# Thirteen tiny DRAM-to-DRAM copies ahead of the loads of a streaming pooling kernel

## The chip, the cores and the metric

The kernel runs on one core of one Trainium2 chip. A core has several engines with instruction queues of their own; this kernel uses ScalarE (ACT in the profile), VectorE (DVE) and SyncE (SP), and 16 DMA engines that move data between DRAM and the on-chip memory. The metric is the device time of one execution in microseconds. Three runs of the kernel before took 394.58, 394.63 and 394.68 us; the median is 394.63 us.

## The reference

The input `x` has the shape 32 x 256 x 4096 in 32-bit floats (134.2 MB), and the output 32 x 256 x 1024 (33.6 MB). Every four neighbouring elements of the last axis give one output, the root of the mean of their squares (p is 2, the window is 4 wide, and windows do not overlap):

```python
for i in range(out_length):
    window = np.abs(x[:, :, i * 4:i * 4 + 4]) ** p
    result[:, :, i] = np.mean(window, axis=-1) ** (1.0 / p)
```

## The kernel before

The whole input is treated as one long row of numbers. It is cut into seven blocks, and each block into 128 equal rows, one for each partition of the on-chip memory. A block's rows are read by up to four loads, of 13184 columns each (52736 bytes for each partition, 6592 KB in all); there are 20 loads, numbered 0 to 19, the last one a little narrower. Three input tiles (`xt`, 128 x 13184) are used in turn, so load i+3 goes into the tile that load i held.

What is done with a load: ScalarE squares it in place in two halves (`square`, L101). VectorE adds pairs (`pairs`, L107) and then the pair sums (`fours`, L111), which leaves a quarter of the columns in a PSUM tile (`st`). ScalarE takes the root of it with a scale of 1/4 (`root`, L114) into the output tile `ot`. When all the loads of a block are done, one store (L98) writes `ot` to the block's rows of the output. The roots of a load come between the squares of the next one. The last two loads are cut finer, so that little is left to do when the last data arrive.

The order on each engine is the order of the Python program (`manual_schedule`): the framework adds the waits and moves nothing. Loads are issued by SP, in order. Load i+3 is issued when the sums of load i are done, since it overwrites them. The stores of the first four blocks are issued by ACT from its own instruction stream, the last three by SP. So two DMA queues are in use: q1 holds what SP issued, and q10 what ACT issued.

Load 0 is split. Its first 1024 columns (`EARLY`) are issued by ACT and the other 12160 by SP. Loads 1 and 2 follow at once on SP and wait for nothing. ACT then runs a table load and a root of a one-column tile, `first`, and waits for load 0.

One thing is not seen in the source. The framework gives each DMA one of eight completion semaphores, in the order of the program and across both queues (the built program names them DMAHW0 to DMAHW7). A DMA that takes a semaphore again first makes its issuing engine wait until the last DMA on that semaphore has completed. In the kernel before, the first eight DMAs (the two parts of load 0, loads 1 to 5 and the first store) each take a fresh one. Every later reuse comes long after the earlier DMA has landed.

Of the kernel before, what the change touches and what calls it, by code (L numbers as in the profile page):

```python
# [1 line left out]

# [4 lines left out]


@with_exitstack
def kernel(  # L10
    ctx: ExitStack,
    tc: tile.TileContext,
    x: bass.AP,
    p: float,
    kernel_size: int,
    out: bass.AP,
):

    nc = tc.nc

    assert float(p) == 2.0, "kernel specialized for p == 2"
    k = int(kernel_size)  # L30
    assert k == 4, "kernel specialized for kernel_size == 4"

    P = nc.NUM_PARTITIONS
    fp32 = mybir.dt.float32
    Act = mybir.ActivationFunctionType
    add = mybir.AluOpType.add
    xf = x.rearrange("b c l -> (b c l)")
    of = out.rearrange("b c l -> (b c l)")
    total = xf.shape[0] // P

    W = 13184
    H, R = W // 2, W // k
    X_SLOTS = 3
    EARLY = 1024
    LAST = total - 19 * W
    widths = [W] * 19 + [LAST]
    n = len(widths)
    assert 0 < LAST <= W and LAST % 16 == 0


    blocks = [[0, 1, 2, 3], [4, 5, 6, 7], [8, 9, 10, 11], [12, 13], [16, 17, 14, 15], [18], [19]]
    block_of = {i: b for b, loads in enumerate(blocks) for i in loads}
    block_width = [sum(widths[i] for i in loads) for loads in blocks]

    x_pool = ctx.enter_context(tc.tile_pool(name="x_pool", bufs=1))
    o_pool = ctx.enter_context(tc.tile_pool(name="o_pool", bufs=1))
    s_pool = ctx.enter_context(tc.tile_pool(name="s_pool", bufs=1, space=bass.MemoryType.PSUM))
    x_tiles = [x_pool.tile([P, W], fp32, name=f"xt{j}") for j in range(X_SLOTS)]
    o_tile = o_pool.tile([P, 4 * R], fp32, name="ot")
    first = o_pool.tile([P, 1], fp32, name="first")  # L60
    s_tiles = [s_pool.tile([P, 2048], fp32, name=f"st{j}") for j in range(2)]
    ctx.enter_context(tc.manual_schedule())

    def rows(flat, b, div):
        at = sum(block_width[:b]) * P // div
        return flat[at:at + block_width[b] * P // div].rearrange("(p w) -> p w", p=P)


    place = {}
    for b, loads in enumerate(blocks):  # L70
        for q, i in enumerate(loads):
            if i < 18:
                place[i] = o_tile[:, q * R:(q + 1) * R]
    free = x_tiles[17 % X_SLOTS]
    place[18] = free[:, 0:R]
    place[19] = free[:, R:R + LAST // k]

    xs = {}

    def load(i):  # L80
        b = block_of[i]
        at = sum(widths[j] for j in blocks[b][:blocks[b].index(i)])
        xs[i] = x_tiles[i % X_SLOTS][:, 0:widths[i]]
        cuts = [0, widths[i]] if i else [0, EARLY, W]
        queues = [nc.sync] if i else [nc.scalar, nc.sync]
        for queue, c, e in zip(queues, cuts, cuts[1:]):
            queue.dma_start(out=xs[i][:, c:e], in_=rows(xf, b, 1)[:, at + c:at + e])  # L87

    def store(b, queue):
        if b <= 2:  # L90
            held = o_tile[:, :]
        elif b == 3:
            held = o_tile[:, 0:2 * R]
        elif b == 4:
            held = o_tile[:, :]
        else:
            held = place[blocks[b][0]]
        queue.dma_start(out=rows(of, b, k), in_=held)  # L98

    def square(v):  # L100
        nc.scalar.activation(out=v, in_=v, func=Act.Square)  # L101

    def pairs(v):

        q = v.rearrange("p (n j) -> p n j", j=k)
        h = v[:, 0:v.shape[1] // 2].rearrange("p (n j) -> p n j", j=2)
        nc.vector.tensor_tensor(out=h, in0=q[:, :, 0:2], in1=q[:, :, 2:4], op=add)  # L107

    def fours(o, v):
        h = v[:, 0:v.shape[1] // 2].rearrange("p (n j) -> p n j", j=2)  # L110
        nc.vector.tensor_tensor(out=o, in0=h[:, :, 0], in1=h[:, :, 1], op=add)  # L111

    def root(o, s):
        nc.scalar.activation(out=o, in_=s, func=Act.Sqrt, scale=1.0 / k)  # L114

    def roots(i):
        for c in range(2):
            root(place[i][:, c * R // 2:(c + 1) * R // 2], s_tiles[c][:, 0:R // 2])
        if i in (3, 7, 11, 13):
            store(block_of[i], nc.scalar)  # L120

    for i in range(X_SLOTS):
        load(i)

    nc.vector.memset(first[:, :], 1.0)  # L125
    root(first[:, :], first[:, :])
    for i in range(18):
        halves = [xs[i][:, c * H:(c + 1) * H] for c in range(2)]
        waits = i > 1 and (i - 1) % 4 == 0
        square(halves[0])  # L130
        if i and not waits:
            roots(i - 1)
        square(halves[1])
        if waits:
            roots(i - 1)
            for v in halves:
                pairs(v)
            for c, v in enumerate(halves):
                fours(s_tiles[c][:, 0:R // 2], v)
        else:  # L140
            for c, v in enumerate(halves):
                pairs(v)
                fours(s_tiles[c][:, 0:R // 2], v)
        if i + X_SLOTS < n:
            load(i + X_SLOTS)
    roots(17)


    c = 5560
    v = xs[18][:, 0:c]  # L150
    nc.vector.tensor_tensor(out=v, in0=v, in1=v, op=mybir.AluOpType.mult)  # L151
    square(xs[18][:, c:W])
    store(4, nc.sync)
    for a, b in ((0, c), (c, W)):
        pairs(xs[18][:, a:b])
        fours(place[18][:, a // k:b // k], xs[18][:, a:b])
    ends = [0, 6912, 10064, LAST]
    for a, b in zip(ends, ends[1:]):
        v = xs[19][:, a:b]
        o = place[19][:, a // k:b // k]  # L160
        square(v)
        if a == 0:
            root(place[18], place[18])
            store(5, nc.sync)
        pairs(v)
        fours(o, v)
        if a:
            root(*last)
        last = (o, o)
    root(*last)  # L170
    store(6, nc.sync)


# [1 line left out]
_INS = ['x', 'p', 'kernel_size']  # L175
_OUTS = [((32, 256, 1024), 'float32')]

_NUMBERS = {'p': 2.0, 'kernel_size': 4}


# [26 lines left out]
```

## Time and profile before

| what | value |
|---|---|
| median of the three runs | 394.63 us |
| span of the profiled execution, first to last instruction | 392.7 us |
| runs' median less this span | 1.9 us |
| ScalarE busy | 279.3 us (71% of the span) |
| VectorE busy | 223.4 us (57%) |
| q1, SP's DMAs | 143.62 MB, 84.9% of the 16 DMA engines' time |
| q10, ACT's DMAs | 24.15 MB, 14.2% |

The profiled execution has no separate time but its span; the runs stand 1.9 us above it, and that is what lies around the first and last instruction. A line of the profile gives engine busy time, a group of equal instructions with its mean duration, or, for DMA, the packets of a queue and the time that they took as a share of 16 engines' time. A window of the profile restricts such a view to a stretch of the span, with times in us from the span's start. A packet is counted in the window in which it starts. In this kernel a packet is one partition's row of one DMA, or the 4-byte write that reports the end of a DMA on one DMA engine.

### The profile page before, as it was taken

How to read it: one execution, taken by the hardware profiler on the slowest of the kernel's cores; microseconds unless marked ns; L12 is line 12 of the kernel's file. 1: busy time of each engine (PE TensorE's matmuls, PEld its weight loads, DVE VectorE, ACT ScalarE, POOL GpSimd, SP SyncE). 2: the span in 40 equal slices, each digit the busy share in tenths (PEclk: the TensorE clock that was granted, in tenths of full speed). 3: DMA queues.
4: the chain of work that ended last, by engine and by line, in shares of the span. 5: the costliest groups of instructions: out<-in, count | busy, mean ns of one | idle time of the engine just before them, and what ended most of it. 6: DMA issues, size and time to landing. Idle time of an engine off the chain costs nothing.

```text
span 392.7 us, 311 instructions
## 1 busy us (share of the span) xinstructions
DVE 223.4 (57%) x84; ACT 279.3 (71%) x82; POOL 0.2 (0%) x4
## 2 busy tenths in 40 slices
DVE  0046586766460567664606667645166654669992
ACT  1095988987650999876419898773297929897792
POOL 0000000000000000000000000000000000000000
DMA  8999999999999999999999999999999999999997
GB/s 337 436 430 430 430 440 440 435 457 376 430 430 430 446 430 440 430 440 440 446 430 436 435 435 431 435 430 430 430 430 419 457 414 430 435 429 451 415 428 320
DMA packets 4034, 167.79 MB, mean 427 GB/s; under 512 B 448, under 2 KB 448, under 8 KB 576
## 3 DMA queue, kind: packets, MB, share of 16 engines
q1 hardware_dynamic: 3312, 143.62, 84.9%
q10 hardware_dynamic: 720, 24.15, 14.2%
q14 instruction: 2, 0.02, 0.0%
HBM read 134.22 MB, written 33.55 MB: 427 GB/s over the span
## 4 chain that ended last, share of the span: by engine, by line
DMA 73%; ACT 17%; DVE 6%; issue 2%; SPq 0%; ACTq 0%; DVEq 0%
DMA xt<-in_x_dram 46%; DMA out_dram<-ot 27%; ACT xt L101 12%; ACT ot L114 5%; DVE xt L107 3%; DVE st L111 2%; DVE xt L111 1%; ACT xt L114 1%; SPq L87 0%; ACTq L101 0%; DVEq L107 0%; ACTq L114 0%
## 5 line engine op out<-in xcount | busy, mean ns | idle before, releaser
L101 ACT ACTIVATE xt<-xt 128x6592 f32<-128x6592 f32 (+4 forms) x40 | 221.4, 5547 | 61.2 <-DMA xt<-in_x_dram 59.6
L107 DVE TENSOR_TENSOR xt<-xt 128x3296 f32<-128x3296 f32 (+5 forms) x41 | 143.1, 3489 | 125.0 <-ACT xt L101 124.7
L111 DVE TENSOR_TENSOR st<-xt 128x1648 f32<-128x1648 f32 x36 | 67.4, 1882 | 36.0 <-ACT ot L114 34.1
L114 ACT ACTIVATE ot<-st 128x1648 f32<-128x1648 f32 x36 | 53.5, 1536 | 43.1 <-DMA out_dram<-ot 40.3
L111 DVE TENSOR_TENSOR xt<-xt 128x1390 f32<-128x1390 f32 (+4 forms) x5 | 7.3, 1452 | 0.2
L114 ACT ACTIVATE xt<-xt 128x3296 f32<-128x3296 f32 (+3 forms) x4 | 6.0, 1492 | 1.1 <-DVE xt L111 1.1
L151 DVE TENSOR_TENSOR xt<-xt 128x5560 f32<-128x5560 f32 x1 | 5.9, 5942 | 0.0
L114 ACT ACT_TABLE_LOAD x1 | 1.3, 1283 | 1.2 <-PEq L188 1.2
L125 DVE MEMSET first<- 128x1 f32 x1 | 0.1, 59 | 0.8 <-PEq L188 0.8
L114 ACT ACTIVATE first<-first 128x1 f32<-128x1 f32 x1 | 0.2, 202 | 0.0
L188 POOL MEMSET const-bfloat16-1.0<- 128x1 bf16 x1 | 0.1, 102 | 0.0
L188 POOL MEMSET const-uint8-127<- 128x1 uint8 x1 | 0.1, 102 | 0.0
L188 POOL MEMSET const-float32-0.0<- 128x1 f32 x1 | 0.1, 99 | 0.2 <-issue 0.2
L188 POOL MEMSET const-float32-1.0<- 128x1 f32 x1 | 0.1, 99 | 0.0
## 6 DMA issues: line engine op xcount, KB each, us to landing
xt<-in_x_dram SPq DMA_DIRECT2D x18, 6592.0 KB, 34.0
out_dram<-ot ACTq DMA_DIRECT2D x3, 6592.0 KB, 35.4
out_dram<-ot SPq DMA_DIRECT2D x1, 6592.0 KB, 24.8
xt<-in_x_dram SPq DMA_DIRECT2D x1, 6080.0 KB, 18.7
xt<-in_x_dram SPq DMA_DIRECT2D x1, 5824.0 KB, 25.2
out_dram<-ot ACTq DMA_DIRECT2D x1, 3296.0 KB, 27.7
out_dram<-xt SPq DMA_DIRECT2D x1, 1648.0 KB, 10.5
out_dram<-xt SPq DMA_DIRECT2D x1, 1456.0 KB, 5.8
```

Of the source, the lines that this page charges most:

```text
L101: nc.scalar.activation(out=v, in_=v, func=Act.Square)
L107: nc.vector.tensor_tensor(out=h, in0=q[:, :, 0:2], in1=q[:, :, 2:4], op=add)
L111: nc.vector.tensor_tensor(out=o, in0=h[:, :, 0], in1=h[:, :, 1], op=add)
L114: nc.scalar.activation(out=o, in_=s, func=Act.Sqrt, scale=1.0 / k)
L125: nc.vector.memset(first[:, :], 1.0)
L151: nc.vector.tensor_tensor(out=v, in0=v, in1=v, op=mybir.AluOpType.mult)
L188: nc = _bacc.Bacc("TRN2", target_bir_lowering=False, num_devices=1)
```

## The change

Load 0 is no longer split: SP issues all its 13184 columns as one DMA. Ahead of the loads ACT issues thirteen copies from `x` straight to the output in DRAM. The copy with n lines (n from 4 to 16) takes 128 columns (512 bytes) from each of the first n rows of the input's first block and writes them to n rows of the output's first block. The columns differ from copy to copy. The store of that block, much later, overwrites all these places with the results, and waits for the copies that it overwrites.

```diff
-    EARLY = 1024
+    TOUCH = 128
...
-        cuts = [0, widths[i]] if i else [0, EARLY, W]
-        queues = [nc.sync] if i else [nc.scalar, nc.sync]
-        for queue, c, e in zip(queues, cuts, cuts[1:]):
-            queue.dma_start(out=xs[i][:, c:e], in_=rows(xf, b, 1)[:, at + c:at + e])
+        nc.sync.dma_start(out=xs[i], in_=rows(xf, b, 1)[:, at:at + widths[i]])
...
+    def touch(lines):
+        to = rows(of, 0, k)[0:lines, (lines - 1) * TOUCH:lines * TOUCH]
+        nc.scalar.dma_start(out=to, in_=rows(xf, 0, 1)[0:lines, (lines - 1) * TOUCH:lines * TOUCH])
+
+    for lines in range(4, 17):
+        touch(lines)
     for i in range(X_SLOTS):
         load(i)
```

There are now sixteen DMAs ahead of everything else, so the eight semaphores are used twice there. The built program orders them as follows (copy n is the copy with n lines). Copy 4 takes DMAHW0, load 0 takes DMAHW1, copies 5 to 10 take DMAHW2 to DMAHW7. Copy 11 takes DMAHW0 again, and ACT waits for copy 4 before it issues it. Copy 12 takes DMAHW1, and ACT waits for load 0. Copies 13 to 16 take DMAHW2 to DMAHW5 behind copies 5 to 8. Load 1 takes DMAHW6, and SP waits for copy 9. Load 2 takes DMAHW7, and SP waits for copy 10. The order of the instructions on VectorE and on the other engines is unchanged.

## The prediction

> **What bounds the kernel now.** I read the page first: the busy shares, the 40 slices and the queues.
>
> ```profile
> span 392.7 us, 311 instructions
> DVE 223.4 (57%) x84; ACT 279.3 (71%) x82; POOL 0.2 (0%) x4
> DMA  8999999999999999999999999999999999999997
> GB/s 337 436 430 430 430 440 440 435 457 376 430 430 430 446 430 440 430 440 440 446 430 436 435 435 431 435 430 430 430 430 419 457 414 430 435 429 451 415 428 320
> q1 hardware_dynamic: 3312, 143.62, 84.9%
> q10 hardware_dynamic: 720, 24.15, 14.2%
> ```
>
> The two queues together fill 99.1% of the 16 DMA engines' time. No compute engine is near that. A change moves the end if it adds DMA work, leaves the DMA engines without work, or takes away one of the few places where they run slowly. Such places stand in the DMA view, in windows that hold just one row for each of the 16 engines. The first below is the start, the second an undisturbed stretch at 90 us, the third the moment when the first store joins the loads (ACT issued it at 90.42).
>
> ```profile
> DMA packets 16, 0.78 MB, mean 324 GB/s; under 512 B 0, under 2 KB 0, under 8 KB 0
> q1 hardware_dynamic: 16, 0.78, 103.2%
> ```
>
> ```profile
> DMA packets 16, 0.84 MB, mean 703 GB/s; under 512 B 0, under 2 KB 0, under 8 KB 0
> q1 hardware_dynamic: 16, 0.84, 162.9%
> ```
>
> ```profile
> DMA packets 16, 0.84 MB, mean 703 GB/s; under 512 B 0, under 2 KB 0, under 8 KB 0
> q1 hardware_dynamic: 16, 0.84, 224.5%
> ```
>
> The windows are 1.7 to 4.1, 89.95 to 91.15 and 91.9 to 93.1 us. A share times the window's length is the time of one row: 103.2% of 2.4 is 2.48 us for the first rows (48640 bytes), 162.9% of 1.2 is 1.95 us for an undisturbed row (52736 bytes), 224.5% of 1.2 is 2.69 us for the rows beside the first store's start. So the start stretches the first row by 0.68 us (at the undisturbed rate 48640 bytes take 1.80), and the first store costs each engine about 0.74 us, once: later stores show no such stretch.
>
> Next, how two queues share an engine, in the window from 4.2 to 17.5 us, where ACT's part of load 0 (4096-byte rows) and SP's run together:
>
> ```profile
> q1 hardware_dynamic: 112, 5.45, 94.7%
> q10 hardware_dynamic: 111, 0.45, 8.3%
> ```
>
> 112 rows of q1 and 111 of q10: an engine takes one packet from each queue in turn, though those of q10 are twelve times smaller. One of them takes 8.3% of 16 x 13.3 us over 111, which is 0.16 us.
>
> Last the timeline of the start, and SP's waits up to 40 us:
>
> ```profile
> 0.73 0.41 ACTq L87 DMA_DIRECT2D xt<-in_x_dram  x1
> 0.73 36.08 SPq L87 DMA_DIRECT2D xt<-in_x_dram  x4
> 1.17 1.28 ACT L114 ACT_TABLE_LOAD   x1 [1.17 <-PEq L188]
> 2.47 0.20 ACT L114 ACTIVATE first<-first 128x1 f32<-128x1 f32 x1
> 19.59 11.28 ACT L101 ACTIVATE xt<-xt 128x6592 f32<-128x6592 f32 x2 [16.92 <-DMA xt<-in_x_dram]
> ```
>
> ```profile
> SPq L87 <- DMA xt<-in_x_dram: 17.5, 1, 17.5
> ```
>
> SP issues loads 0, 1 and 2 back to back from 0.73 us. It then waits for load 0 (the 17.5 us) and for its sums, and issues load 3 at about 36.4. Loads 1 and 2 are thus in q1 long before load 0 has landed, and the engines go from one to the next without a hole.
>
> **The change, part by part.**
>
> *The early piece goes.* Its 8 rows on each engine cost 0.16 us each against 4096 / 52736 x 1.95 = 0.15 within a longer row, and one report packet less: about -0.1 us on every engine.
>
> *The copies as DMA work.* No row of before is a 512-byte copy. From below one costs its bytes at the row rate, 0.02 us; from above the 0.16 us of a 4096-byte row. I take 0.03, near the lower end, since it is an eighth of that row. 130 data packets and as many reports over 16 engines are 8 of each for an engine: +0.3 us (0.2 to 1.4). An engine that gets all 13 copies pays 0.4. What comes before load 1 on an engine is paid inside the hole described next; I count 0.1.
>
> *Load 1's new wait.* This is the largest term. Load 1 takes the completion semaphore of copy 9, so SP issues it only when copy 9 has landed, and load 2 stands behind it on SP. ACT issues copies 4 to 10 at 0.41 us each, from 0.73 to about 3.6, so all of them are in the rings when load 0's first rows end at 4.2 to 5.2 us. If copy n lies on n engines, one row each, and always from the same first engine, the first four engines hold all of them: up to copy 9, six data packets and six reports, 12 packets. Alternating with load 0's eight rows and its report, they need more turns than load 0 offers. Copy 9 then ends just behind load 0 on these engines. Before, the reports of load 0 fall between 17.98 and 19.02 us by engine, 18.35 in the mean, and the first four engines, which start first, are among the earliest, at 18.0 to 18.25. So copy 9 is written at about 18.35. From report to waiting engine: the last report of load 0 starts at 19.02 and ACT starts at 19.59, and two later loads show 0.4 to 0.5; I take 0.45. SP issues load 1 at 18.8. From issue to first packet the start shows 1.02 us (0.73 to 1.75); the first rows then start over 0.9 us, 1.3 us after the issue in the mean, and are stretched by 0.68. An engine is back at full rate, counted as if at once, at 18.8 + 1.3 + 0.7 = 20.8 us, where before it went on at 18.35: +2.45 us. Nothing covers this, for q1 holds only load 0 until then. Bounds: 1.3 if the second start shows no stretch and no spread of starts; 3.2 if copies stretch the first engines by as much as the first store does (0.74), since all engines then wait for these four.
>
> *ACT's new waits.* Copy 12 waits for load 0, at about 19.5. Behind it on ACT stand four more copies, the table load, the root of `first` and the first square. Five issues of 0.34 to 0.41, 1.28 and 0.20: the square starts at about 22.9 instead of 19.59. VectorE follows, and load 3's issue goes from 36.4 to 39.7. Load 2's rows keep the engines busy until about 52, and load 1 lands only at about 37, when ACT is done with load 0 (34.3). Cost nothing; if the cover were gone it would be 3.3 us. The waits of loads 3 to 7 for copies 11 to 16 end long before, as these drain within some ten rows, by about 41.
>
> *The first store's stretch.* The copies write to the output before it, on every engine. If the stretch belongs to the first write to that tensor, up to 0.74 us goes at 92 us, less what the copies pay for it. If it belongs to reading `ot`, nothing goes. I take half, -0.4 (0 to -0.74). Later waits for stores and loads shift with the loads.
>
> Sum: -0.1 + 0.1 + 2.45 - 0.4 = +2.05 us against the profiled 392.7; the 1.9 us around the span stay, so 394.63 becomes 396.7.
>
> The Trainium skill, "DMA: Bandwidth & Descriptors", section "Queues, rings and completion order", says that an engine drains a packet of about 9 to 17 descriptors from one ring before it turns to the next. By that the copies would be through after a row or two, load 1 would be issued in time, and the sum would lose its 2.45. The alternation above, one row each, speaks against it. Section "Why a DMA increments its semaphore by 16 and not by 1" of the same page gives a DMA of n rows from SP or ACT the lowest-numbered n engines for such n; no row here shows that, and it speaks for the wait as I counted it.
>
> **The rivals.**
>
> *No hole.* The copies get through earlier: their first engine moves on from copy to copy, so that the 39 rows of copies 4 to 9 give an engine two or three rows and their reports, some six turns or 12 us, or small packets pass several at a time. Load 1 is then issued before 13 us. Against it only the row-by-row alternation; where copies of few rows lie, no row shows. Time: 394.63 - 0.1 + 0.3 - 0.4, about 394.4 (393.9 to 395.0).
>
> *Faster.* The same early finish, and the whole stretch of 0.74 goes because the copies take it over while the engines still wait for data in the first 1.75 us. It decides only if copy 9 ends before about 17 us. Price -0.74 - 0.1 + 0.1: about 393.9, and 393.7 if the end also falls more evenly on the engines. For it: the stretch occurs only once, on the first store. Against it: copies 11 to 16 go out while loads run.
>
> *A longer hole.* The copies' first writes stretch the four engines before copy 9 by 0.74 or more, or a small copy costs more than a 4096-byte row. Load 1 goes out about 0.8 us later and the late engines get a stretch of their own: 2.45 + 0.8, with no gain at 92 us: about 397.9.
>
> **How the numbers follow.** Forecast 0.68 (396.7, own range 395.8 to 397.4), longer hole 0.11, no hole 0.16, faster 0.05. A measurement tells a change of over 0.2%, or 0.8 us, from none. Slower by that are the forecast and the longer hole, 0.79; within it, no hole and a part of the faster case, 0.17; faster 0.04. The range goes from 394.9, into the no-hole case, to 398.1.
>
> **What would show it.** In the profile after, SP's second load is issued at about 18.8 us instead of about 1.1, the DMA slices show a hole around 19 to 20 us with a second set of stretched first rows, the first square starts near 22.9, and load 1's square near 37 instead of 35.02; later loads land some 2 to 2.5 us later. The window at the first store shows whether its 2.69 us a row has gone to 1.95. If SP's second issue stands before 17 us, the forecast is wrong; then the sum is that of the rivals without a hole.

## The result and the profile after

The changed kernel takes 398.01 us (397.67 to 398.31), the kernel before 394.65 us in the same comparison. The ratio is 1.0082, with a 95% interval from 1.0069 to 1.0094: slower by 3.4 us. The forecast was slower by 2.05 us, to 396.7 us, with a range from 394.9 to 398.1.

The page of the kernel after shows the loss in one place, near the front: of the 40 slices of the span only the second (7 tenths busy) stands below its value of before (9 tenths).

```profile
span 396.4 us, 328 instructions
DMA  8799999999999999999999999999999999999997
GB/s 341 343 423 433 426 426 426 426 426 426 426 426 426 426 426 426 452 436 474 426 426 422 426 431 426 426 431 452 452 442 394 442 447 426 431 426 447 411 430 317
q1 hardware_dynamic: 3312, 144.15, 84.6%
q10 hardware_dynamic: 836, 23.69, 13.8%
```

That slice (9.9 to 19.8 us) moves 343 GB/s, where the kernel before had 436. Nothing later is lower than before by as much. The chain that ended last (start, duration, what) tells what the stretch waited for:

```profile
5.04 0.03 issue
5.07 14.50 DMA out_dram<-in_x_dram
19.57 0.02 issue
19.59 18.38 DMA xt<-in_x_dram
```

At 5.07 us ACT issues copy 9 (the copy with nine lines). It lands 14.50 us later, although it moves 4.5 KB, and at 19.59 SP issues load 1. SP's own waits up to 60 us name the same thing, 18.5 us behind a copy, where before the first wait was 17.5 us for load 0, with loads 1 and 2 already issued:

```profile
SPq L84 <- DMA out_dram<-in_x_dram: 18.5, 1, 18.5
```

What that does to the DMA engines stands in two windows of the DMA view, 18.82 to 20.68 us and 20.8 to 21.9 us:

```profile
DMA packets 0, 0.00 MB, mean 0 GB/s; under 512 B 0, under 2 KB 0, under 8 KB 0
```

```profile
q1 hardware_dynamic: 16, 0.84, 231.8%
q10 hardware_dynamic: 7, 0.00, 0.6%
```

For 1.86 us not one packet starts on any of the 16 engines. Then load 1's first 16 rows start, and 231.8% of 1.1 us is 2.55 us for each instead of 1.95, so the first row after the hole is stretched by 0.6 us. The timeline shows the compute side (ACTq and SPq lines are DMA issues, with the waits between them):

```profile
0.73 57.34 SPq L84 DMA_DIRECT2D xt<-in_x_dram  x5
0.73 22.42 ACTq L121 DMA_DIRECT2D out_dram<-in_x_dram  x13
23.18 1.28 ACT L111 ACT_TABLE_LOAD   x1 [23.18 <-DMA out_dram<-in_x_dram]
24.58 11.27 ACT L98 ACTIVATE xt<-xt 128x6592 f32<-128x6592 f32 x2
37.98 5.70 ACT L98 ACTIVATE xt<-xt 128x6592 f32<-128x6592 f32 x1 [2.14 <-DMA xt<-in_x_dram]
```

The kernel before has this line for its first square of load 1:

```profile
35.02 5.70 ACT L101 ACTIVATE xt<-xt 128x6592 f32<-128x6592 f32 x1 [4.14 <-DMA xt<-in_x_dram]
```

ACT is held by its copies until 23.15 us and squares load 0 at 24.58 instead of 19.59, 5.0 us late. But at load 1 it waits for data again (37.98 instead of 35.02), so from there on the data are late, by 3.0 us, and not ACT. Last, the rows beside the first store's start (ACT issued it at 93.33), in the window from 95.55 to 96.1 us:

```profile
q1 hardware_dynamic: 16, 0.84, 514.9%
```

514.9% of 0.55 us is 2.83 us a row, as against 2.69 before: the stretch at the first store has not gone.

### The profile page after: what moved, and what is told of

It is laid out like the page before. It is cut to its first block, busy times and chain, and to the rows that moved or that the text cites. A ratio compares the mean times of both kernels' runs of the same rounds, so it can differ in the third digit from the quotient of the medians.

```text
span 396.4 us, 328 instructions
## 1 busy us (share of the span) xinstructions
DVE 223.3 (56%) x84; ACT 279.4 (70%) x82; POOL 0.2 (0%) x4
## 4 chain that ended last, share of the span: by engine, by line
DMA 72%; ACT 17%; DVE 6%; issue 2%; ACTq 1%; SPq 0%; DVEq 0%
DMA xt<-in_x_dram 42%; DMA out_dram<-ot 26%; ACT xt L98 11%; ACT ot L111 5%; DMA out_dram<-in_x_dram 4%; DVE xt L104 3%; DVE st L108 2%; ACTq L121 1%; DVE xt L108 1%; ACT xt L111 1%; ACTq L98 0%; ACTq L111 0%; SPq L84 0%; ACTq L95 0%; DVEq L104 0%
```

## The experiments

The theory: the copies themselves cost next to nothing; what costs is that load 1 takes the completion semaphore of a copy that cannot land before load 0's rows are through, so the DMA engines run empty. The rivals: the copies cost as such (their writes, or their place on a few engines), and ACT's late start costs. All kernels but those derived from the kernel before are the changed kernel with the edit shown. Ratios are against the kernel before, with 95% intervals.

### The wait without any copy

```diff
-    for lines in range(4, 17):
-        touch(lines)
-    for i in range(X_SLOTS):
+    load(0)
+    nc.sync.dma_start(out=rows(of, 0, k)[:, 0:128], in_=xs[0][:, 0:128])
+    for i in range(1, X_SLOTS):
         load(i)
```

> No tiny copies at all; SP issues load 0, then one small store of 128 rows of 512 bytes that reads load 0's tile and so waits for load 0, then loads 1 and 2. Theory (load 1's late issue is the cost): load 1 goes out at about 19.5 to 20 us, the DMA engines stand empty as in the changed kernel, 397.6 to 398.6 us. Rival (the copies themselves, their writes or their place on the first engines cost the time): no copies, no cost, 394.4 to 395.0 us.

Measured: 398.35 us, ratio 1.0086 (1.0071 to 1.0102). With no copy at all the loss is that of the changed kernel. Its chain:

```profile
0.72 18.19 DMA xt<-in_x_dram
18.91 0.02 issue
18.93 0.34 SPq L124
19.27 0.05 issue
19.32 18.44 DMA xt<-in_x_dram
```

The small store waits for load 0 until 18.93, and load 1 goes out at 19.32. This speaks for the theory and excludes that the copies are needed for the loss. The small store has a side effect, since ACT may overwrite load 0 only when it has been read: the first square starts at 20.56 instead of 19.59. A delay of that size is covered, as the late copies below show.

### The wait twice

```diff
-    for i in range(1, X_SLOTS):
-        load(i)
+    load(1)
+    nc.sync.dma_start(out=rows(of, 0, k)[:, 128:256], in_=xs[1][:, 0:128])
+    load(2)
```

(an edit of the kernel above)

> As the kernel without copies in which a small store that reads load 0 holds load 1 back (3.7 us over before), with a second such store, reading load 1, ahead of load 2. Theory (each wait for a load to land costs one empty stretch of the DMA engines plus one stretched first row): a second hole near 38 us, 401.2 to 402.2 us. Rival (the loss belongs to the start and is paid once): 398.2 to 399 us.

Measured: 401.31 us, ratio 1.0162 (1.0147 to 1.0177): another 2.96 us, for a wait far from the start. The trace has the second hole, here in the window from 37.4 to 38.54 us:

```profile
DMA packets 0, 0.00 MB, mean 0 GB/s; under 512 B 0, under 2 KB 0, under 8 KB 0
```

So the loss belongs to DMA queues that have run empty, not to the start of the kernel.

### Another copy to wait for

```diff
-    for lines in range(4, 17):
+    for lines in range(4, 13):
```

> Copies 4 to 12 only, everything else as in the changed kernel. Load 1 now waits for copy 5 and load 2 for copy 6; copy 12 on ACT still waits for load 0. Theory (what counts is which copy load 1 waits for): copy 5 lands after some four turns, near 11 us, load 1 is in the ring before load 0's rows end, no hole, 394.5 to 395.2 us. Rival (copies cost as such): 9 of 13 copies, or 72 of 130 rows, 396.5 to 397.0 us. Rival (ACT's late first square is what costs): ACT is still some 2 us late, 395.7 to 396.3 us.

Measured: 394.97 us, ratio 1.0006 (0.9996 to 1.0015). Four copies fewer change which copy load 1 waits for, and no loss is left that can be told. The chain, and ACT's timeline:

```profile
1.99 10.79 DMA out_dram<-in_x_dram
12.78 0.01 issue
12.79 22.00 DMA xt<-in_x_dram
```

```profile
0.73 19.00 ACTq L121 DMA_DIRECT2D out_dram<-in_x_dram  x9
21.17 11.27 ACT L98 ACTIVATE xt<-xt 128x6592 f32<-128x6592 f32 x2
34.81 5.70 ACT L98 ACTIVATE xt<-xt 128x6592 f32<-128x6592 f32 x1 [2.38 <-DMA xt<-in_x_dram]
```

Copy 5 was issued at 1.99 and lands at 12.78, and load 1 is issued at 12.79, some five microseconds before load 0's rows end. ACT still squares load 0 late, at 21.17, and load 1 lands as early as before (34.81; before 35.02). Both rivals expected 395.7 us or more.

### Copies without a second use of a semaphore

```diff
-    for lines in range(4, 17):
+    for lines in range(12, 17):
```

> Copies 12 to 16 only: 70 rows, on every engine, and with the three loads just eight DMAs, so no semaphore is taken twice and neither SP nor ACT waits for a copy. Theory: no hole, 394.5 to 395.0 us, and the stretch of the rows at the first store (2.7 to 2.9 us instead of 1.95) is still there, as in the changed kernel. Rival (copies cost as such): 70 of 130 rows, 396.2 to 396.6 us. Rival (copies take over the first store's stretch): 393.9 to 394.2 us.

Measured: 394.69 us, ratio 0.9999 (0.9989 to 1.0009). 70 of the 130 copied rows, on every engine, cost nothing that can be told, and they do not take over the first store's stretch either: by the trace's packet records the rows near 92 us are stretched by 0.83 us for each engine in the mean, before by 0.86.

### All thirteen copies, but late

```diff
-    for lines in range(4, 17):
+    for lines in range(4, 9):
         touch(lines)
...
         square(halves[0])
+        if i == 0:
+            for lines in range(9, 17):
+                touch(lines)
```

> All thirteen copies, but copies 9 to 16 stand on ACT behind the first square. Load 1 takes a fresh semaphore and waits for nothing; load 2 waits for copy 9, which lands near 30 us, before load 1's rows end; copy 16 waits for load 1, so ACT's second square is issued only near 36 us, some 11 us late. Theory (only an empty ring costs time, and ACT's lateness is covered): no hole, load 3 still in time, 394.6 to 395.4 us. Rival (130 rows of copies cost as such): 397.5 to 398.3 us. Rival (ACT's lateness costs): 400 us or more.

Measured: 395.04 us, ratio 1.0024 (0.9995 to 1.0053). Nine of the ten runs lie between 394.87 and 395.31 us; the tenth took 400.47 us, which widens the interval and is not explained, since the trace is of another run (394.92 us). The timeline of ACT shows how late it was:

```profile
18.95 16.19 ACTq L121 DMA_DIRECT2D out_dram<-in_x_dram  x8
35.19 11.28 ACT L98 ACTIVATE xt<-xt 128x6592 f32<-128x6592 f32 x2 [10.55 <-DMA out_dram<-in_x_dram]
```

The second half of load 0 is squared at 35.19, where before it followed the first half at about 25.3. ACT stood still for 10.55 us in the middle of its work, and in the median the kernel lost 0.3 us. SP issued load 3, which waits for the sums of load 0, at 46.49 us instead of 36.48, but load 2 lands only at 50.1, so the engines still had rows to move. So the cover that the prediction named for ACT's delay is real, and it is deeper than the 5 us that the changed kernel asks of it.

### The other half of the change alone

```diff
-    for lines in range(4, 17):
-        touch(lines)
```

> The other half of the change alone: load 0 as one DMA on SP, no copies. Theory: one report and eight small packets less on each engine, 0.1 us less, 394.4 to 394.7 us. Rival (the split helped the start): 395.0 to 395.6 us.

Measured: 394.68 us, ratio 0.9997 (0.9988 to 1.0006). Load 0 in one piece is worth nothing that can be told.

### What the first store's stretch belongs to

These four are edits of the kernel before. Each adds one early DMA to the first block of the output.

```diff
+    early = o_pool.tile([P, 128], fp32, name="early")
...
+    nc.vector.memset(early[:, :], 1.0)
+    nc.scalar.dma_start(out=rows(of, 0, k)[:, 0:128], in_=early[:, :])
```

> The kernel before with one small early store on ACT's queue, 128 rows of 512 bytes from an on-chip tile of ones into the first block of the output, overwritten later. It asks whether the one-off stretch of rows at the first real store goes when every engine has read the on-chip memory and written the output from ACT's queue before. If so: the rows at 92 us take 1.95 us and the time is 393.9 to 394.3 us. If not (the small copies did not remove it either, so this is the likelier): still 2.7 to 2.9 us a row there, 394.6 to 395.0 us.

Measured: 394.79 us, ratio 1.0003 (0.9993 to 1.0012). In the window from 92.1 to 93.0 us the rows take 298.6% of 0.9, 2.69 us:

```profile
q1 hardware_dynamic: 16, 0.84, 298.6%
```

```diff
+    nc.vector.memset(o_tile[:, 0:1024], 1.0)
+    nc.scalar.dma_start(out=rows(of, 0, k)[:, 0:1024], in_=o_tile[:, 0:1024])
```

> The kernel before with an early store on ACT's queue of 128 rows of 4096 bytes from the output tile, filled with ones there: 8 packets of 0.16 us on each engine, 1.3 us, taken from all partitions and not from 16. If 4096-byte rows are enough to take over the one-off stretch, the rows at 92 us take 1.95 us and the time is 395.3 to 396.0 us; if not, 395.7 to 396.2 us with 2.7 us a row there.

Measured: 395.80 us, ratio 1.0033 (1.0020 to 1.0045). The stretch is still there: from 93.05 to 93.8 us, 365.8% of 0.75 is 2.74 us a row.

```profile
q1 hardware_dynamic: 16, 0.84, 365.8%
```

```diff
+    nc.vector.memset(o_tile[0:16, :], 1.0)
+    nc.scalar.dma_start(out=rows(of, 0, k)[0:16, :], in_=o_tile[0:16, :])
```

> The kernel before with an early store on ACT's queue of 16 full rows of 52736 bytes (one for each engine) from the output tile, filled with ones there, overwritten later. One row more on each engine costs 1.95 us. If the stretch belongs to the first store with large rows, it moves to this store and the rows at 92 us take 1.95 us: about 396.6 us. If it belongs to the large store of all 128 rows joining the loads: it stays at 92 us, also about 396.6 us; the trace tells them apart, not the time.

Measured, in two runs: 400.43 us, ratio 1.0141 (1.0121 to 1.0162), 4 us more than expected. Two windows, 20.2 to 20.95 us (the early store's rows) and 98.6 to 100.55 us (the loads' rows when the first real store joins; ACT issued it at 97.11):

```profile
q10 hardware_dynamic: 16, 0.84, 787.4%
```

```profile
q1 hardware_dynamic: 16, 0.84, 100.0%
```

The stretch is gone from the first real store (100.0% of 1.95 us). But the sixteen early rows took 787.4% of 0.75, 5.9 us each, and the extra time is mostly theirs.

```diff
+    nc.scalar.dma_start(out=rows(of, 0, k)[0:16, :], in_=rows(xf, 0, 1)[0:16, 0:4 * R])
```

> The kernel before with one copy on ACT's queue of 16 full rows of 52736 bytes from the input straight to the first block of the output, overwritten later; one row more on each engine, 1.95 us. If the one-off stretch at 92 us belongs to the first long writes to DRAM, whatever they are read from, it goes from 92 us to this copy: about 396.6 us, rows at 92 us 1.95 us. If it belongs to the first long rows read from on-chip memory, it stays at 92 us: about 396.6 us too; the trace tells them apart.

Measured: 396.76 us, ratio 1.0060 (1.0040 to 1.0080). From 19.85 to 20.8 us and from 94 to 95 us:

```profile
q10 hardware_dynamic: 16, 0.84, 204.9%
```

```profile
q1 hardware_dynamic: 16, 0.84, 234.8%
```

The copied rows take 204.9% of 0.95, 1.95 us, as any row. At the first real store a row takes 2.35 us: stretched, but less than the 2.69 of before. Neither expectation holds as it was written. What the four say together: early rows of 512 and of 4096 bytes do not take the stretch over, early rows of 52736 bytes do, in full (from on-chip memory) or in part (from DRAM). Whether it belongs to the write to DRAM, to the read from on-chip memory or to both together is not settled.

No version found beats the kernel before by more than can be told.

## Why the prediction was right, point by point

The direction, the place and the mechanism were right; the size was short by 1.3 us of 3.36. The measured 398.01 us lies outside the forecast's own range (395.8 to 397.4) and inside the whole range by only 0.1 us: its upper end, 398.1, reaches past the longer hole's 397.9. That the number fell inside is in part luck. By the steps of the sum:

*The early piece, -0.1 us.* The kernel without copies stands at 0.9997 (0.9988 to 1.0006). A tenth of a microsecond cannot be told from this.

*The copies as DMA work, +0.1 us.* By the trace's packet records most copies take 27 ns a row, where 0.03 us was taken, and the five-copy kernel loses nothing. Right. Their issue on ACT was mis-sized: the 0.41 us of a 128-row load was taken for each, and the profile has 0.57 to 1.27 us, 0.77 at the median. This changed little for load 1: copy 9's issue ended at 5.84 us, long before load 0 did.

*Load 1's wait, +2.45 us.* This term was mis-sized: it measured about 3.4 us, above its upper bound of 3.2. Load 1 was issued at 19.59 instead of 18.8 us. Part of that is that copy 9 ended later on the engines. The prediction took the first engines to end load 0 among the earliest, at 18.0 to 18.25 us; by the trace's packet records, strung together by end and start, one engine that holds copies 4 to 11 ended its rows of load 0 only at 18.65, and copy 9's report started there at 18.74, behind the copies before it. The other part is the time from that report to the issue of load 1, about 0.85 us, where 0.45 had been read from loads. From the issue to the first row it took 1.22 us instead of 1.02, and to the rows' start in the mean 1.54 instead of 1.3; the second stretch, 0.6, was nearly as forecast (0.7). So an engine is back at full rate at 19.59 + 1.54 + 0.60 = 21.7 us, 0.9 us later than the 20.8 of the prediction. Load 0's reports fall between 17.90 and 18.80 us, 18.35 in the mean, as before; the difference is the 3.4. The kernel with the wait and without copies loses 3.66 us by the runs.

*Where the copies lie.* The prediction took all copies to start on the same engine. The trace's record of the semaphores bears it out: copy 9's semaphore rises once just after its issue and then nine times, copy 5's once and then five times. Copy 5's first of these five comes at 9.1 us, the other four at 12.5 to 13.1: one engine is free of copy 4, four are not. This agrees with the Trainium skill, "DMA: Bandwidth & Descriptors", section "Why a DMA increments its semaphore by 16 and not by 1": there the issuing engine counts the unused DMA engines at once, each used one adds 1 when its data have landed, and the used ones are the lowest-numbered. By the rule of the same page's section "Queues, rings and completion order", a packet of some 9 to 17 descriptors from one ring at a time, copy 9 would by estimate have landed within a row or two. It took 14.50 us, and the packet records show one packet of ACT's queue between two rows of load 0, so here the measurement decides.

*ACT's delay, nothing.* It was 5.0 us instead of 3.3, because of the longer issues, and covered: the late copies held ACT for 10.55 us at no cost to speak of.

*The first store's stretch, -0.4 us.* This step failed. It was taken as half a gain, because the copies write to the output on every engine before the store does. The rows there took 2.83 us in place of 2.69. The other kernels whose early writes are small, or that have none, keep the stretch too: by the packet records 0.64 to 0.98 us for each engine, 0.92 in the changed kernel and 0.86 before. So the copies gave nothing back.

The two misses, 0.9 and 0.4 us, make the difference between 2.05 and 3.36. Of the rivals, the one without a hole and the faster one are excluded by SP's second issue at 19.59 us. The longer hole came nearest in size (397.9 us), but not by its mechanism. It had load 1 go out 0.8 us later, as it did, but because the copies' first writes stretch the engines or a copy costs more than a 4096-byte row. By the packet records none of the 130 copied rows took more than 0.031 us, and the rows beside them took 1.95. What it also had right is that nothing is gained at the first store.

## What to carry to other kernels

A DMA costs more than its bytes: it takes a completion semaphore, and where those are few and handed round (eight here), a large load can come to wait for a tiny transfer that has nothing to do with it. Before adding small DMAs ahead of a stream, count the DMAs until the first one that reuses a semaphore, look at which earlier transfer it must wait for, and ask when that one ends; with nine copies instead of thirteen the same code lost nothing that can be told. In this kernel, whose DMA engines are always full, one load that is issued only after the one before has landed costs 3.0 to 3.7 us (three kernels), while a compute engine that was 10.55 us late cost 0.3 us.

## What the runs showed of the hardware that was not expected

A copy of 4 to 16 rows from DRAM to DRAM kept ACT's instruction stream busy with its issue for 0.57 to 1.27 us; the 128-row loads of the kernel before took 0.33 to 0.42 us. A copy of 4.5 KB took 14.50 us to land, as its packets took turns with rows of 52736 bytes, one by one. Sixteen long rows read from sixteen neighbouring partitions at the same time took 5.9 us each, against 1.95 us for sixteen such rows copied from DRAM and for the rows of a full store. The first store with long rows stretched the rows beside it once, by 0.6 to 1.0 us for each engine; early long rows took this over in full or in part, small ones did not.
